# Causal pooling of three channel groups by transposes and doubled sums on VectorE in place of band products on TensorE, and a 0/1 product moved behind the inverses

## The chip, the cores and the metric

The kernel runs on one core of a Trainium2 chip. The metric is the device time of one execution in microseconds. Several executions are timed and their median is given; one more execution is taken by the hardware profiler, and all views of the profile and of its trace come from that one. Engines are named as in the profile: PE is TensorE (PEld its weight load), DVE is VectorE, ACT is ScalarE, POOL is GpSimd, SP is SyncE, which here issues most DMAs.

## What is computed

One layer of a decoder on 256 tokens of 2048 channels, float32 in and out. The part around the change is the token mixer: a normalised x is projected by `w_in` into q, k, v, z, two gates and a pooling input `p_in`. q, k and v go through a convolution over time and into a gated delta rule of 16 heads, whose output is `y_a`. The pooling input is cut into four groups of 512 channels with windows of 2, 4, 8 and 16 tokens:

```
def causal_multiscale_pool(u):          # u: (B, S, G, Cg)
    for gi, win in enumerate((2, 4, 8, 16)):
        hi = cs[:, 1:, gi]              # running sum up to t
        lo = cs[:, max(t + 1 - win, 0), gi]
        cnt = min(t + 1, win)
        outs.append((hi - lo) / cnt)
    return pooled - u                   # trailing mean minus the token itself

y_b   = einsum('bsgc,gcd->bsgd', pooled, pool_w) * pool_scale
mixed = sigmoid(g_a) * y_a + sigmoid(g_b) * y_b
x     = x + mixed @ w_out
```

After it come a second norm, a gated MLP with 5632 hidden channels and a last norm. They are not touched.

## The kernel before, in words

Large products. Every float32 weight is split into a high and a low part, so that three products of fp32r operands stand for one product in fp32. `weights()` gives out weight tiles of 256 x 512 (128 partitions x 1024) in one fixed order: the SP queue loads `raw` (L124, four buffers), ScalarE casts it to `whi` (L143, three buffers) and VectorE subtracts to get `wlo` (L151, three buffers), two tiles ahead of their use. `gemm_a` (L170) takes one tile per step and issues twelve products for it (L181 to L183), into `psm`, a PSUM tile with two buffers. Each step is two half-steps, and after each half-step it calls `side()`, which advances a generator of side work by one `yield`. The list `later` holds closures that `gemm_a` runs at its second step (c == 1): work on the result of the product before.

Order of a group. A loop over four groups g (L864), each with four heads and 512 pooling channels, runs these large products one after another: K, Q, V, P (the pooling input), GB (gate of the pooling branch), the pool product with `pool_w` (L916, two weight tiles), Z and GA. The result of P is evicted by ScalarE with the row scale into `e` (tag `ev`, one buffer, tokens on partitions), and `pooled` (L894) is put on `later`, so that it is traced at the second step of GB. The pool product needs its results `phi` and `plo` (high and low part, channels on partitions) as the stationary operand.

Pooling before. `pooled` multiplies `e` by a band matrix: `bands[:, g]` holds 1/win (1/count at the start, from `icnt`) on a band and subtracts the identity, all halved. For each pair of 128-channel blocks TensorE makes two fp32 products per block (L899 of 128 columns and L901 of 144), into a `psg` tile; ScalarE casts it to `phi` (L904) and VectorE subtracts to get `plo` (L905). `psg` is a PSUM tag with four buffers of one bank each, shared by all small products. `fixed_parts` (L534) builds the bands of all groups once, on GpSimd and VectorE, during group 0.

Side work. The generator `gdn` (L634) does the delta rule of a group: decay matrices, Gram products of k and q (L673, L675; two `psg` tiles per head, read by VectorE at L678 and L692 to L697), a way through DRAM for the 32 x 32 diagonal blocks (`cdd`, `lb`, L710 to L714), squares of q (L718), their block transpose and sum on VectorE (L722, L725), a product with a 0/1 matrix `sel` that sums them over partitions (L729) and four short VectorE operations that make `ro` of it (L733). After a fixed count of yields (`WAIT`, `LATE`) the inverses of the diagonal blocks follow on VectorE, a chain of 62 short operations (L744, L746) that reads `lb`, then a second way through DRAM (L751, L754), and then the products that merge the blocks and make the output (L788 to L847). `ro` is used near the end (L857). In group 3 the generator waits in a loop of yields (L769) until the last large product nears its end.

What sets the order. The kernel is traced under a tile framework (`TileContext(nc, schedule_with_timeline_sim=True)`), which tracks the dependences of tiles, hands out buffers and orders the instructions of each engine before the run by a simulated timeline; what is traced earlier goes first among what is ready. Within an engine the order is then fixed. Two stretches have an order on TensorE that is written out by hand: the start and the end of the mixer (L318, L926).

## Time and profile before

| what | value |
|---|---|
| median of 3 executions | 1565.36 us (1564.85 to 1565.47) |
| the profiled execution | 1565.06 us |
| its span in the trace | 1563.3 us |
| granted TensorE clock, mean | 0.998 |
| VectorE in the stretch 300.2 to 314.5 us | 10.51 us busy of 14.3 |
| VectorE in the stretch 476.5 to 493.5 us | 13.27 us busy of 17.0 |

The span is what the trace shows from the first to the last instruction; the profiled execution's own time is 1.8 us longer. A row of a timeline gives the start, the time from the first start to the last end, the engine, the line, the operation, output and inputs, the tile's shape and how often it follows itself. Successive matmuls overlap in the trace, so what one costs TensorE is read from the distance of starts. In the groups' rows stand the total busy time and the mean in ns of one, then the engine's idle time just before them with what ended it. Group 0 of the loop above lies between about 33 and 184 us, and the groups follow each other at about 179 us.

### The profile page before, as it was taken

Reading aid. Unit: us, or ns where it says so; the run is one execution under the profiler, and the core shown is the slowest. Engines: PE = TensorE matmul, PEld = TensorE weight load, DVE = VectorE, ACT = ScalarE, POOL = GpSimd, SP = SyncE. Lnnn points to the kernel's source line nnn. Section 1 sums busy time; section 2 is a strip of 40 time slices with the busy share of each in tenths; the row PEclk is TensorE's granted clock in tenths of the full one; section 3 lists DMA queues with packets and bytes.
Section 4 is the critical chain, followed back from the end, with each engine's and each line's share of the span. In section 5 each row is a group of like instructions: output and inputs, shape, how many; then the busy total and the mean of one; then the engine's idle time right before and its main releaser. Section 6 shows DMA issues by size and latency. Waiting matters only on the chain.

```text
span 1563.3 us, 21270 instructions
## 1 busy us (share of the span) xinstructions
PE 1554.1 (99%) x8008; PEld 1306.1 (84%) x8008; DVE 1085.6 (69%) x1702; ACT 745.7 (48%) x958; POOL 41.3 (3%) x69
## 2 busy tenths in 40 slices
PE   9999999999999999999999999999999999999997
PEld 8878888888888888888888888888888888888886
DVE  6898758896698848886656666776666667444444
ACT  6545445454554445354544544444444444333443
POOL 2110000000000001000000000000000000000000
PEclk9999999999999999999999999999999999999999
DMA  8676657676676656676656666666666666666662
GB/s 273 200 222 207 194 162 212 201 208 178 182 221 198 194 152 201 210 209 184 212 180 177 196 187 188 188 190 188 187 184 195 188 188 214 197 191 210 200 223 91
DMA packets 168229, 304.23 MB, mean 195 GB/s; under 512 B 19234, under 2 KB 22834, under 8 KB 167998
## 3 DMA queue, kind: packets, MB, share of 16 engines
q1 hardware_dynamic: 165104, 297.84, 64.0%
q10 hardware_dynamic: 3022, 5.03, 0.9%
q8 instruction: 63, 1.03, 0.3%
q14 instruction: 40, 0.33, 0.1%
HBM read 297.56 MB, written 5.27 MB: 194 GB/s over the span
## 4 chain that ended last, share of the span: by engine, by line
PE 99%; issue 1%; ACT 0%; DVE 0%; POOL 0%; POOLq 0%
PE psm L183 15%; PE psm L181 15%; PE psm L182 15%; PE psm L205 10%; PE psg L205 10%; PE psg L206 5%; PE psm L206 5%; PE psg L1058 3%; PE psg L1060 2%; PE psg L1059 2%; PE psm L1059 2%; PE psm L1060 2%; PE psm L1058 2%; PE psm L312 1%; PE psg L673 1%; PE psg L226 1%
## 5 line engine op out<-in xcount | busy, mean ns | idle before, releaser
L151 DVE TENSOR_TENSOR wlo<-raw,whi 128x1024 fp32r<-128x1024 f32 x522 | 636.7, 1223 | 374.1 <-ACT whi L143 371.2
L143 ACT CAST whi<-raw 128x1024 fp32r<-128x1024 f32 x524 | 551.1, 1053 | 715.7 <-PE psm L182 314.9
L183 PE MATMUL psm<-wlo,xhl 128*128 128x512 f32 x864 | 339.8, 393 | 0.0
L182 PE MATMUL psm<-whi,xhl 128*128 128x512 f32 x864 | 338.9, 392 | 0.0
L181 PE MATMUL psm<-whi,xhl 128*128 128x512 f32 x864 | 338.0, 391 | 0.0
L205 PE MATMUL psm<-fhl,whi 128*128 128x512 f32 x704 | 246.2, 396 | 0.0
L205 PE MATMUL psg<-fhl,whi 128*128 128x512 f32 x704 | 238.0, 394 | 0.0
L206 PE MATMUL psm<-fhl,wlo 128*128 128x256 f32 x704 | 194.4, 279 | 0.0
L183 PEld LDWEIGHTS psm<-wlo,xhl 128*128 128x128 f32 x864 | 162.3, 188 | 33.1
L182 PEld LDWEIGHTS psm<-whi,xhl 128*128 128x128 f32 x864 | 162.2, 188 | 33.1
L181 PEld LDWEIGHTS psm<-whi,xhl 128*128 128x128 f32 x864 | 162.2, 188 | 32.7
L206 PE MATMUL psg<-fhl,wlo 128*128 128x256 f32 x704 | 178.7, 279 | 0.0
L205 PEld LDWEIGHTS psm<-fhl,whi 128*128 128x128 f32 x704 | 131.4, 188 | 30.5
L205 PEld LDWEIGHTS psg<-fhl,whi 128*128 128x128 f32 x704 | 129.2, 188 | 24.2
L206 PEld LDWEIGHTS psg<-fhl,wlo 128*128 128x128 f32 x704 | 132.5, 188 | 6.9
L206 PEld LDWEIGHTS psm<-fhl,wlo 128*128 128x128 f32 x704 | 132.5, 188 | 1.1
L1058 PE MATMUL psg<-whi,hhi 128*128 128x512 f32 x168 | 65.5, 390 | 0.0
L1059 PE MATMUL psg<-whi,hlo 128*128 128x512 f32 x168 | 65.4, 389 | 0.0
L1058 PE MATMUL psm<-whi,hhi 128*128 128x512 f32 x168 | 65.4, 389 | 0.0
L1059 PE MATMUL psm<-whi,hlo 128*128 128x512 f32 x168 | 65.4, 389 | 0.0
L1060 PE MATMUL psm<-wlo,hhi 128*128 128x512 f32 x168 | 65.4, 389 | 0.0
L1060 PE MATMUL psg<-wlo,hhi 128*128 128x512 f32 x168 | 59.0, 389 | 0.0
(267 smaller groups left out, 1519.0 us busy)
## 6 DMA issues: line engine op xcount, KB each, us to landing
raw<-in_w_in_dram SPq DMA_DIRECT2D x224, 512.0 KB, 4.3
raw<-in_w_up_dram SPq DMA_DIRECT2D x176, 512.0 KB, 4.5
raw<-in_w_down_dram SPq DMA_DIRECT2D x88, 512.0 KB, 4.4
raw<-in_w_out_dram SPq DMA_DIRECT2D x32, 512.0 KB, 4.7
mv<-vrow SPq DMA_DIRECT2D x12, 512.0 KB, 5.6
taps<-in_conv_qkv_w_dram SPq DMA_DIRECT2D x16, 256.0 KB, 5.1
raw<-in_pool_w_dram SPq DMA_DIRECT2D x8, 512.0 KB, 4.5
vrow<-ev SPq DMA_DIRECT2D x4, 512.0 KB, 3.0
```

The costliest lines, as they stand in the source:

```text
L143: nc.scalar.copy(hi, raw)
L151: last_split[0] = nc.vector.tensor_tensor(lo, raw, hi.bitcast(F32), op=ALU.subtract).ins
L181: mm(ps[:, t, :], lh(k, t), hi[:, kk, :], start=(k == 0), stop=False)
L182: mm(ps[:, t, :], ll(k, t), hi[:, kk, :], start=False, stop=False)
L183: mm(ps[:, t, :], lh(k, t), lo[:, kk, :], start=False, stop=(k == nk - 1))
L205: mm(ps[f], hi[:, kk, fs], rhl(k), start=(k == 0), stop=False, skip_group_check=True)
L206: mm(ps[f][:, 1, :], lo[:, kk, fs], rhl(k)[:, 0, :], start=False, stop=(k == nk - 1), skip_group_check=True)
L226: nc.tensor.transpose(pt[:, ff, t * P : (t + 1) * P], src[:, t, f * P : (f + 1) * P], ident)
L312: mm(ps_k0[:, t, :], part(k, t), w[:, kk, :], start=(k == 0 and w is hi and part is xh), stop=(k == KD - 1 and w is lo))
L1058: mm(acc[c][t], lh(k, t), hi[:, kk, :], start=(k == 0), stop=False)
L1059: mm(acc[c][t], ll(k, t), hi[:, kk, :], start=False, stop=False)
L1060: mm(acc[c][t], lh(k, t), lo[:, kk, :], start=False, stop=(k == KF - 1))
```

## The change

For groups 0 to 2, `pooled` no longer multiplies by bands. It turns `e` by eight TensorE transposes into two `psg` tiles (`turned`, L218, the helper that the convolution uses too), ScalarE copies them to `u` (tag `pu`), and VectorE makes the window's sum by doubling: each step adds the running sum to itself shifted by n tokens, n = 1, 2, 4, while ScalarE copies the first n columns. One addition for a window of 2, two for 4, three for 8. Then VectorE multiplies the first `win` columns by 1/count, subtracts u there, and does the rest in one operation (sum/win - u); ScalarE casts the whole to `phi`, VectorE subtracts to get `plo`. Sums alternate between a new tag `pa` and the buffer that `plo` gets afterwards. Since the bands' factor of a half is gone, `e` is evicted with the halved row scale in these groups. Group 3 (window 16) keeps the band products, as `banded`, and `bands` holds its matrix alone. `plo` is allocated when the closure runs, and handed on in a list.

In `gdn`, the product with `sel` and the four operations of `ro` move from ahead of the wait for the inverses to behind the second way through DRAM, with one `yield` more after them. The tile `bat` at the start takes another tag.

```diff
--- before.py
+++ after.py
@@ -443,7 +443,6 @@
     for g, w in enumerate(WINDOWS):
         nc.vector.tensor_scalar(icnt[:, g, :], tio, float(w), None, op0=ALU.min)
     nc.vector.reciprocal(icnt, icnt)
-    nc.vector.tensor_scalar(icnt, icnt, 0.5, None, op0=ALU.mult)
     idh = mp.tile([P, P], F32, name="idh")
     nc.vector.tensor_scalar(idh, ident, 0.5, None, op0=ALU.mult)
 
@@ -464,7 +463,7 @@
         for kk in range(8):
             k = 8 * c + kk
             mm(pba, hi[:, kk, :], xhl[:, k], start=(k == 0), stop=(k == KD - 1))
-    bat = mp.tile([64, 2, S], F32, tag="u", name="bat")
+    bat = mp.tile([64, 2, S], F32, tag="w2", name="bat")
     nc.vector.tensor_copy(bat, pba[:64])
     pbt = pg([P, 2, 32])
     for t in range(2):
@@ -526,24 +525,23 @@
 
 
 
-    bands = mp.tile([P, 4, NB], F32, name="bands")
+    bands = mp.tile([P, NB], F32, name="bands")
 
     Ta = mp.tile([P, 8, P], F32, name="T")
     TTa = mp.tile([P, 8, P], F32, name="TT")
 
     def fixed_parts():
-        for g, win in enumerate(WINDOWS):
-            bd = bands[:, g, :]
-            nc.gpsimd.memset(bd, 0.5 / win)
-            nc.vector.tensor_copy(bd[:, 0:PAD], icnt[:, g, :])
-            for cs in (slice(0, P + PAD), slice(P + PAD, NB)):
-                b = bd[:, cs]
-                n = cs.stop - cs.start
-                nc.gpsimd.affine_select(b, b, pattern=[[1, n]], compare_op=ALU.is_ge, fill=0.0, base=0,
-                                        channel_multiplier=-1)
-                nc.gpsimd.affine_select(b, b, pattern=[[-1, n]], compare_op=ALU.is_ge, fill=0.0, base=win - 1,
-                                        channel_multiplier=1)
-                nc.vector.tensor_tensor(b[:, 0:P], b[:, 0:P], idh, op=ALU.subtract)
+        win = WINDOWS[3]
+        nc.gpsimd.memset(bands, 0.5 / win)
+        nc.vector.tensor_scalar(bands[:, 0:PAD], icnt[:, 3, :], 0.5, None, op0=ALU.mult)
+        for cs in (slice(0, P + PAD), slice(P + PAD, NB)):
+            b = bands[:, cs]
+            n = cs.stop - cs.start
+            nc.gpsimd.affine_select(b, b, pattern=[[1, n]], compare_op=ALU.is_ge, fill=0.0, base=0,
+                                    channel_multiplier=-1)
+            nc.gpsimd.affine_select(b, b, pattern=[[-1, n]], compare_op=ALU.is_ge, fill=0.0, base=win - 1,
+                                    channel_multiplier=1)
+            nc.vector.tensor_tensor(b[:, 0:P], b[:, 0:P], idh, op=ALU.subtract)
         nc.gpsimd.memset(Ta, 0.0)
         nc.gpsimd.memset(TTa, 0.0)
 
@@ -725,13 +723,6 @@
         nc.vector.tensor_reduce(qp.rearrange("p (h c) -> p h c", h=4), qx.rearrange("p h (c j) -> p h c j", j=32), axis=mybir.AxisListType.X,
                                 op=ALU.add)
         yield
-        pn = pg([P, 4, 2, 4])
-        mm(pn.rearrange("p h t c -> p (h t c)"), sel.rearrange("p b i -> p (b i)"), qp, start=True, stop=True)
-        ro = mp.tile([P, 2, 4], F32, tag="ro", name=nm("ro"))
-        for c in range(4):
-            pr = slice(32 * c, 32 * c + 32)
-            nc.vector.tensor_scalar(ro[pr], pn[pr, :, :, c].rearrange("p h t -> p t h"), EPS * P, EPS * EPS * P,
-                                    op0=ALU.mult, op1=ALU.add)
         for _ in range(WAIT - 3 + LATE[g]):
             yield
         tb = mp.tile([P, 8, B0], F32, tag="tb", name=nm("tb"))
@@ -752,6 +743,14 @@
         for r in range(NR):
             rs = slice(B0 * r, B0 * (r + 1))
             nc.sync.dma_start(TTa[rs, :, rs], tbd.rearrange("(q r) a (c i) -> r (a c) q i", q=8, i=B0)[r])
+        pn = pg([P, 4, 2, 4])
+        mm(pn.rearrange("p h t c -> p (h t c)"), sel.rearrange("p b i -> p (b i)"), qp, start=True, stop=True)
+        ro = mp.tile([P, 2, 4], F32, tag="ro", name=nm("ro"))
+        for c in range(4):
+            pr = slice(32 * c, 32 * c + 32)
+            nc.vector.tensor_scalar(ro[pr], pn[pr, :, :, c].rearrange("p h t -> p t h"), EPS * P, EPS * EPS * P,
+                                    op0=ALU.mult, op1=ALU.add)
+        yield
 
         for _ in conv:
             yield
@@ -887,24 +886,50 @@
         win = WINDOWS[g]
         psb = scales(g)
         ps = gemm_a(xh, xl, KD)
-        e = evict(ps)
+        e = evict(ps) if g == 3 else evict(ps, rsh)
         phi = mtile(g, [P, 4, S], F32R, nm("phi"))
-        plo = mtile(4 + g, [P, 4, S], F32R, nm("plo"))
-
-        def pooled(e=e, g=g, phi=phi, plo=plo):
+        plo = []
+
+        def banded(e=e, g=g, phi=phi, plo=plo):
+            plo.append(mtile(4 + g, [P, 4, S], F32R, nm("plo")))
             for f2 in range(2):
                 pt = pg([P, 2, S])
                 for ff in range(2):
                     fs = slice((2 * f2 + ff) * P, (2 * f2 + ff + 1) * P)
-                    mm(pt[:, ff, P:S], e[:, 1, fs], bands[:, g, P + PAD : NB], start=True, stop=False,
+                    mm(pt[:, ff, P:S], e[:, 1, fs], bands[:, P + PAD : NB], start=True, stop=False,
                        skip_group_check=True)
-                    mm(pt[:, ff, 0 : P + PAD], e[:, 0, fs], bands[:, g, 0 : P + PAD], start=False, stop=True,
+                    mm(pt[:, ff, 0 : P + PAD], e[:, 0, fs], bands[:, 0 : P + PAD], start=False, stop=True,
                        skip_group_check=True)
                 fs = slice(2 * f2, 2 * f2 + 2)
                 nc.scalar.copy(phi[:, fs, :], pt)
-                nc.vector.tensor_tensor(plo[:, fs, :], pt, phi[:, fs, :].bitcast(F32), op=ALU.subtract)
-
-        later.append(pooled)
+                nc.vector.tensor_tensor(plo[0][:, fs, :], pt, phi[:, fs, :].bitcast(F32), op=ALU.subtract)
+
+        def pooled(e=e, g=g, win=win, phi=phi, plo=plo):
+
+
+            u = mp.tile([P, 4, S], F32, tag="pu", name=nm("pu"))
+            for f2, pt in enumerate(turned(e)):
+                nc.scalar.copy(u[:, 2 * f2 : 2 * f2 + 2, :], pt)
+            src, n = u, 1
+            while n < win:
+                if n * 4 == win:
+                    dst = mp.tile([P, 4, S], F32, tag="pa", name=nm("pa"))
+                else:
+                    dst = mtile(4 + g, [P, 4, S], F32, nm("pb"))
+                nc.scalar.copy(dst[:, :, 0:n], src[:, :, 0:n])
+                nc.vector.tensor_tensor(dst[:, :, n:], src[:, :, n:], src[:, :, : S - n], op=ALU.add)
+                src, n = dst, 2 * n
+            pool = mp.tile([P, 4, S], F32, tag="pa", name=nm("pool"))
+            nc.vector.tensor_tensor(pool[:, :, 0:win], src[:, :, 0:win],
+                                    icnt[:, g, 0:win].unsqueeze(1).to_broadcast([P, 4, win]), op=ALU.mult)
+            nc.vector.tensor_tensor(pool[:, :, 0:win], pool[:, :, 0:win], u[:, :, 0:win], op=ALU.subtract)
+            nc.vector.scalar_tensor_tensor(pool[:, :, win:], src[:, :, win:], 1.0 / win, u[:, :, win:],
+                                           op0=ALU.mult, op1=ALU.subtract)
+            nc.scalar.copy(phi, pool)
+            plo.append(mtile(4 + g, [P, 4, S], F32R, nm("plo")))
+            nc.vector.tensor_tensor(plo[0], pool, phi.bitcast(F32), op=ALU.subtract)
+
+        later.append(banded if g == 3 else pooled)
 
         def gate(ps, tag):
             th = mp.tile([P, 2, 512], F32, tag=tag, name=nm("gate"))
@@ -913,7 +938,7 @@
             return th
 
         tb = gate(gemm_a(xh, xl, KD), "th")
-        ps = gemm_a(lambda k, t: phi[:, k, t * P : (t + 1) * P], lambda k, t: plo[:, k, t * P : (t + 1) * P], 4)
+        ps = gemm_a(lambda k, t: phi[:, k, t * P : (t + 1) * P], lambda k, t: plo[0][:, k, t * P : (t + 1) * P], 4)
         yb = mp.tile([P, 2, 512], F32, tag="yb", name=nm("yb"))
         nc.vector.tensor_tensor(yb, ps, psb.unsqueeze(1).to_broadcast([P, 2, 512]), op=ALU.mult)
         nc.vector.scalar_tensor_tensor(yb, tb, 1.0, yb, op0=ALU.add, op1=ALU.mult)
```

## Prediction

> **What bounds the kernel now.** I read the page from the top first: busy shares, the chain that ended last, and then the waits of TensorE alone.
>
> ```profile
> span 1563.3 us, 21270 instructions
> PE 1554.1 (99%) x8008; PEld 1306.1 (84%) x8008; DVE 1085.6 (69%) x1702; ACT 745.7 (48%) x958; POOL 41.3 (3%) x69
> ...
> PE 99%; issue 1%; ACT 0%; DVE 0%; POOL 0%; POOLq 0%
> ```
>
> ```profile
> PE psm L242 <- POOL ones L232: 1.1, 1, 1.1
> ```
>
> TensorE is busy 99% of the span, the chain that ended last lies on it for 99%, and the only wait of TensorE in the whole list of waits is 1.1 us at the very start. So the time is the sum of what TensorE is given, at the pace at which it takes instructions: a product less is time less, as long as no operand comes late. That pace is read from starts, since the durations of matmuls overlap. I therefore read two places of TensorE's timeline: eight transposes of an `ev` tile between large products, and the banded products of group 2.
>
> ```profile
> 250.53 0.39 PE L183 MATMUL psm<-wlo,xhl 128*128 128x512 f32 x1
> 250.76 1.03 PE L226 MATMUL psg<-ident,ev 128*128 128x128 f32 x8
> 251.55 0.48 PE L181 MATMUL psm<-whi,xhl 128*128 128x512 f32 x1
> 251.86 0.40 PE L182 MATMUL psm<-whi,xhl 128*128 128x512 f32 x1
> ```
>
> ```profile
> 480.71 0.39 PE L182 MATMUL psm<-whi,xhl 128*128 128x512 f32 x1
> 480.94 0.30 PE L729 MATMUL psg<-qp,sel 128*128 128x32 f32 x2
> 481.08 0.47 PE L899 MATMUL psg<-bands,ev 128*128 128x128 f32 x2
> ...
> 481.63 0.38 PE L899 MATMUL psg<-bands,ev 128*128 128x128 f32 x2
> ...
> 482.79 0.41 PE L901 MATMUL psg<-bands,ev 128*128 128x144 f32 x2
> 482.94 0.49 PE L183 MATMUL psm<-wlo,xhl 128*128 128x512 f32 x1
> 483.26 0.39 PE L181 MATMUL psm<-whi,xhl 128*128 128x512 f32 x1
> ```
>
> A large product starts 0.23 us after the one before it (480.71 to 480.94). From the large product ahead of a block to the second one behind it there are two such steps, and the rest is the block's price. Eight transposes: 251.86 - 250.53 = 1.33, less 0.45, is **0.88 us**. The product of q's squares with the banded products: 483.26 - 480.71 = 2.55, less 0.45, is **2.10 us**. Each fp32 product is two instructions here and a transpose is one: 16 against 8.
>
> **The change part by part.**
>
> *Products out, transposes in.* Of the 2.10 us, the product of q's squares (L729) takes 0.14 (480.94 to 481.08) and 0.08 more in the product behind it (0.47 against 0.38): 0.22, which leaves 1.88 for the banded ones. In groups 0 to 2 they go and eight transposes come: 1.88 - 0.88 = 1.00 us each, **3.0 us** in all. Group 3 keeps its bands.
>
> *L729 behind the inverses.* The same two instructions, now alone between large products. The trace has it only ahead of the bands. Bounds: 0.14 us as here, 0.88 us (the eight transposes) as the most. I take 0.22, nearest to its own row, so nothing per group; over four groups the bounds are -0.3 and +2.6. Its four short VectorE operations (ro) move along into the inverse stretch, where they add nothing new; ro is wanted only at the end of the recurrence. The added yield puts the later side work half a weight tile on, and group 3's loop that yields until the tail begins takes it up. No DMA changes its place in the SP queue, except that the value rows' work behind the inverse's transfers is issued one such step later.
>
> *VectorE, ScalarE, GpSimd.* Prices by these rows:
>
> ```profile
> L151 DVE TENSOR_TENSOR wlo<-raw,whi 128x1024 fp32r<-128x1024 f32 x522 | 636.7, 1223 | 374.1 <-ACT whi L143 371.2
> L143 ACT CAST whi<-raw 128x1024 fp32r<-128x1024 f32 x524 | 551.1, 1053 | 715.7 <-PE psm L182 314.9
> ```
>
> ```profile
> L628 DVE SCALAR_TENSOR_TENSOR kq<-th,cy 128x1024 f32<-128x1024 f32 x8 | 9.9, 1240 | 0.3 <-ACT th L627 0.3
> L905 DVE TENSOR_TENSOR plo<-psg,phi 128x512 fp32r<-128x512 f32 x8 | 5.2, 686 | 0.1
> L904 ACT CAST phi<-psg 128x512 fp32r<-128x512 f32 x8 | 4.7, 586 | 4.6 <-PE psg L901 4.6
> L733 DVE TENSOR_SCALAR ro<-psg 32x8 f32<-32x8 f32 x16 | 2.6, 162 | 0.5
> ```
>
> One doubling is 1.22 us (L151's size). The mean is two short operations of some 0.16 (L733) and one of 1.24 (L628), the low part 1.22 in place of two of 0.69. So VectorE gets 1.22n + 0.32 + 1.24 + 1.22 - 1.37 = 1.22n + 1.4 us more, n = 1, 2, 3: 2.6, 3.9 and 5.1. ScalarE copies u in two pieces (0.59 each, as phi before), makes short copies beside the additions (bounded by nothing and 0.59 each) and a phi of 1.05. Both have room over the span (69% and 48%), so none of this is on TensorE's path unless phi or plo is late for the pool product, or the new work holds up the weights queued behind it. Behind u's copies on ScalarE stand weight casts (715.7 us idle before them, mostly for TensorE to hand back a buffer), behind the doublings on VectorE the splits (374.1 us idle, for the casts): that idle time is the cover, and without it each microsecond of chain would be one of TensorE's. The band work that goes at the start was off the path too, by the one wait of 1.1 us.
>
> *Is phi late?* The pool products of groups 0, 1 and 2 begin here, the second with the start of its group's bands:
>
> ```profile
> 135.43 0.39 PE L181 MATMUL psm<-whi,phi 128*128 128x512 f32 x1
> ```
>
> ```profile
> 304.76 0.47 PE L899 MATMUL psg<-bands,ev 128*128 128x128 f32 x2
> ...
> 314.46 0.39 PE L181 MATMUL psm<-whi,phi 128*128 128x512 f32 x1
> ```
>
> ```profile
> 493.50 0.39 PE L181 MATMUL psm<-whi,phi 128*128 128x512 f32 x1
> ```
>
> And this is VectorE ahead of them, in the same order:
>
> ```profile
> 122.72 1.20 DVE L725 TENSOR_REDUCE qp<-kq 128x32 f32<-128x1024 f32 x1
> ```
>
> ```profile
> 299.71 0.48 DVE L697 SCALAR_TENSOR_TENSOR ga<-psg,sj,dec 128x256 f32<-128x256 f32 x1
> ...
> 301.33 1.21 DVE L725 TENSOR_REDUCE qp<-kq 128x32 f32<-128x1024 f32 x1
> 302.46 2.35 DVE L151 TENSOR_TENSOR wlo<-raw,whi 128x1024 fp32r<-128x1024 f32 x2
> ...
> 311.22 0.28 DVE L741 COPY tb<-idb 128x256 f32<-128x256 f32 x1
> 313.12 0.42 DVE L744 TENSOR_TENSOR tmp<-lb,tb 128x248 f32<-128x248 f32 x1 [1.62 <-DMA lb<-cdd]
> ```
>
> ```profile
> 476.03 0.48 DVE L697 SCALAR_TENSOR_TENSOR ga<-psg,sj,dec 128x256 f32<-128x256 f32 x1
> ...
> 477.65 1.21 DVE L725 TENSOR_REDUCE qp<-kq 128x32 f32<-128x1024 f32 x1
> 478.78 2.35 DVE L151 TENSOR_TENSOR wlo<-raw,whi 128x1024 fp32r<-128x1024 f32 x2
> 481.28 0.69 DVE L733 TENSOR_SCALAR ro<-psg 32x8 f32<-32x8 f32 x4
> 482.00 1.23 DVE L151 TENSOR_TENSOR wlo<-raw,whi 128x1024 fp32r<-128x1024 f32 x1
> ...
> 486.40 1.23 DVE L151 TENSOR_TENSOR wlo<-raw,whi 128x1024 fp32r<-128x1024 f32 x1 [1.85 <-ACT whi L143]
> 487.54 0.28 DVE L741 COPY tb<-idb 128x256 f32<-128x256 f32 x1
> ```
>
> The four psg banks are held by the Gram products until L697 reads them. Two are free at 476.5, yet the bands start at 481.08, right behind L729, which needs L725's sums. I read this as L729 holding its turn for a bank ahead of them; with L729 gone, the transposes can go at 476.6. Group 2 then: transposes to 477.4, copies of u to 478.1, VectorE free of L725 at 478.8, three additions, two short operations and the mean in 5.2 us, and up to three weight splits among them, 3.6 us: 487.6. phi on ScalarE to 488.9, plo to 490.1. The pool product starts 1.2 us earlier than before (2.10 - 0.88), at 492.3: **2.2 us to spare**. Group 1 alike from 302.5: 4.0 + 3.6 gives 310.1, phi 311.4, plo 312.6, against 313.3: **0.7 us to spare**. Group 0 has one addition less: from 123.9 its 2.8 + 3.6 give 130.3, plo 132.8, against 134.2. So I forecast no new wait.
>
> **Sum.** The profiled execution took 1565.06 us (span 1563.3 and 1.8 around it), 0.3 under the median of 1565.36. Less 3.0 that is 1562.1, or 1562.4 by the median; I say 1562.2.
>
> **The rivals.**
>
> *The pooled operand is a little late.* If the transposes stay where the bands were (the reading of the banks is wrong, or the order planned for TensorE keeps them there), the chain starts 4 us later: in group 1, from L729's turn at 304.6, u is there at 306.2, four us of chain and two splits end at 312.6, plo at 315.1 against 313.5: 1.6 us late. By the same working groups 0 and 2 lose 0.5 and nothing. Net -3.0 + 2.1: **1564.2**. For it: the row at 313.12, where VectorE stands 1.62 us for the transfer of lb; whatever is queued behind waits too, plo among it. Against it: the banks are free early.
>
> *VectorE's order starves the chain: slower.* VectorE works in order, and inverse, splits and doublings now meet in one stretch. If two other operations come between every two of the chain, it runs at a third of its pace: group 2's 5.2 us become 15.6, phi's low part is there at 496.9 against 492.5; group 1's 12.0 from 302.5 give 317.0 against 313.5; group 0 loses 0.4. TensorE stands 8.3 us: net +5.3, **1570.6**. It decides from 3.0 us of standing, a chain at some 2.2 times its length. For it: the inverse's operations (L741 at 487.54) start inside the stretch already. Against it: at 486.40 VectorE stood 1.85 us for want of a cast, so it was ahead of its work.
>
> *Transposes are no cheaper.*
>
> ```profile
> L226 PE MATMUL psg<-ident,ev x64: 270/272/307, 62.6 to 605.2; 128*128 128x128 f32 x64
> ```
>
> If TensorE paid a transpose's full 0.27 us, eight would take 2.2 us against 1.88, and the time would be 1565.06 + 3 x 0.3 = **1566.0**. The row at 250.76 speaks against it: the next large product starts 0.79 us later. The Trainium skill (TensorE: Matmul & The Clock Gate, Part 4: PE-mode transpose) gives about 275 ns for one in a kernel and says that the clock gate does not count transposes as work. By that figure the change would lose 0.9 us; the trace agrees with it as a duration (272 ns), not as a pace (eight in 1.03 us).
>
> **How the numbers follow.** Forecast: 0.60, 1561.6 to 1562.9 (the bound of -0.3, the median's 0.3, and how side products happen to group). Late operand: 0.17. Starved chain: 0.18. Dear transposes: 0.02. A gain above 3.5 us: 0.03. The range runs from 1561.4 to 1566.0; it leaves out most of the starved chain and a little below. About what a measurement of this kernel can tell from no change is 0.2%, 3.1 us, and 1565.36 - 3.1 = 1562.2 cuts the forecast's own case in two. Faster by more: 0.33 + 0.03 = 0.36. Within: 0.27 + 0.17 + 0.02 and 0.02 of the starved chain, 0.48. Slower by more: 0.16.
>
> **What would show it.** Right: blocks of eight L226 on `ev` in the gate product of groups 0 to 2, at 0.88 us each and some 4 us earlier than the bands; L729 alone, behind the inverses, at 0.2; TensorE's list of waits as short as now; phi done over 1 us before the pool product. Wrong: TensorE waiting at the product that reads phi or plo, or at L183 for a wlo; L744's wait for lb ahead of plo; transposes still at the bands' place.

## The result, and the profile after

The changed kernel takes **1576.86 us** (median of 4 runs, 1575.42 to 1580.69) against 1565.41 us before (1564.85 to 1565.71): 11.45 us more, a ratio of 1.0075 with a 95% interval of 1.0063 to 1.0087. The forecast was 1562.2 us, with a range up to 1566.0. The profiled execution took 1580.69 us. Its page begins:

```profile
span 1579.0 us, 21230 instructions
...
PE 1560.6 (99%) x7984; PEld 1309.0 (83%) x7984; DVE 1092.6 (69%) x1704; ACT 749.0 (47%) x967; POOL 47.3 (3%) x54
...
PE 96%; DMA 2%; DVE 1%; issue 1%; SPq 1%; ACT 0%; POOLq 0%; POOL 0%; DVEq 0%
```

The busy shares are as before. What differs is the chain that ended last: 3% more of it has left TensorE, for a DMA above all. TensorE's list of waits, one row long before, says where:

```profile
PE psm L181 <- ACT phi L928: 3.6, 2, 2.0
PE psg L787 <- DVE T L764: 3.2, 2, 2.5
PE psm L182 <- DVE plo L930: 2.0, 2, 1.0
```

That is 8.8 us of waiting, in three places: ahead of the pool products of groups 1 and 2 (phi, then plo), and ahead of group 3's U product (the first product that reads T, the transposed inverses). Group 1's place in TensorE's timeline (start, duration, line):

```profile
312.35 0.39 PE L183 MATMUL psm<-wlo,xhl 128*128 128x512 f32 x1
314.35 0.50 PE L181 MATMUL psm<-whi,phi 128*128 128x512 f32 x1 [1.62 <-ACT phi L928]
315.87 0.79 PE L182 MATMUL psm<-whi,plo 128*128 128x512 f32 x1 [1.02 <-DVE plo L930]
316.46 0.63 PE L183 MATMUL psm<-wlo,phi 128*128 128x512 f32 x1
316.89 0.63 PE L181 MATMUL psm<-whi,phi 128*128 128x512 f32 x1
```

From start to start there are 2.00 and 1.52 us where 0.23 is the pace: 3.1 us of standing (time in which TensorE has nothing that it could start). Behind it the products do not return to their pace but follow each other at 0.43 us. The stretches of the same time show why (columns: busy time with instructions, granted clock, DMA share, GB/s); first after, then before:

```profile
312.00:316.00 4.00, 1.36 (x6) 0.89 0.67 214
316.00:322.00 6.00, 6.00 (x15) 0.50 0.50 166
322.00:328.00 6.00, 6.00 (x28) 1.00 0.41 126
```

```profile
316.00:322.00 6.00, 6.00 (x28) 1.00 0.66 182
```

15 products in place of 28 in six busy microseconds: the granted clock is at 0.50. In fine stretches it is so from 315.1 to 322.0, from 499.5 to 506.3 and from 731.6 to 738.4: each time 6.8 us. It begins while TensorE still stands (at 315.1, where plo's product starts at 315.87), so a part of it costs nothing. "PE 99%" doesn't show it, for a slow product counts as busy.

Set against before by the starts of the large products, the profiled run's 15.6 us are: group 0, gate product to pool product, -0.95; group 1, gate product to Z, +5.1; group 2 the same, +5.2; group 3, last gate product to output product, +6.3. Adding back the gain of 0.95 in groups 1 and 2 and taking off the standing (3.1, 3.4 and 3.3 us by starts) leaves 3.0, 2.7 and 3.0 us for the half clock. The other runs took 1575.4 to 1577.3, at a mean clock of 0.994 and 0.995 in place of 0.992: an estimated 6 to 9 us less at half clock (0.002 to 0.003 of 1579 us, doubled).

This is VectorE ahead of group 1's pool product, and then SyncE's queue in the same time:

```profile
306.16 1.22 DVE L920 TENSOR_TENSOR pa<-pu 128x1020 f32<-128x1020 f32 x1
307.49 1.22 DVE L920 TENSOR_TENSOR pb<-pa 128x1016 f32<-128x1016 f32 x1
308.62 1.22 DVE L151 TENSOR_TENSOR wlo<-raw,whi 128x1024 fp32r<-128x1024 f32 x1
...
310.04 1.20 DVE L926 SCALAR_TENSOR_TENSOR pool<-pb,pu 128x1008 f32<-128x1008 f32 x1
312.72 0.42 DVE L735 TENSOR_TENSOR tmp<-lb,tb 128x248 f32<-128x248 f32 x1 [1.47 <-DMA lb<-cdd]
313.05 0.17 DVE L925 TENSOR_TENSOR pool<-pool,pu 128x16 f32<-128x16 f32 x1
313.14 1.22 DVE L151 TENSOR_TENSOR wlo<-raw,whi 128x1024 fp32r<-128x1024 f32 x1
314.27 0.41 DVE L737 TENSOR_TENSOR tb<-tb,tmp 128x248 f32<-128x248 f32 x1
314.60 1.22 DVE L930 TENSOR_TENSOR plo<-pool,phi 128x1024 fp32r<-128x1024 f32 x1
```

```profile
304.41 0.39 SPq L124 DMA_DIRECT2D raw<-in_pool_w_dram  x1
304.89 0.41 SPq L124 DMA_DIRECT2D raw<-in_w_in_dram  x1
305.54 1.73 SPq L712 DMA_DIRECT2D lb<-cdd  x4
```

The chain is nearly done at 311.2. But its last piece, the short subtraction of 0.17 us (L925), is queued behind the first operation of the inverse (L735), which stands 1.47 us for lb; then come a split and L737, and only then plo. In group 2 it is the same: L735 stands 1.83 us, with four operations of the pooling behind it. Before the change that wait was there too (1.62 us), with nothing behind it that TensorE was near to needing. And lb, itself four transfers of 128 KB, was fetched behind two weight tiles of 512 KB; it landed 5.6 us after its issue.

The theory to test: lb's wait on VectorE makes phi and plo late; the standing halves the clock; and group 2's longer stretch pushes group 3's T past a place written by hand. Rivals: the moved 0/1 product is to blame; the chain is too long whoever waits in it; the standing of all groups adds up in group 3.

### The profile page after: what moved, and what is told of

It reads as the page before. It is cut to its first block, busy times and chain, and to the rows that moved or that the text cites. A ratio compares the mean times of both kernels' runs of the same rounds, so it can differ in the third digit from the quotient of the medians.

```text
span 1579.0 us, 21230 instructions
## 1 busy us (share of the span) xinstructions
PE 1560.6 (99%) x7984; PEld 1309.0 (83%) x7984; DVE 1092.6 (69%) x1704; ACT 749.0 (47%) x967; POOL 47.3 (3%) x54
## 4 chain that ended last, share of the span: by engine, by line
PE 96%; DMA 2%; DVE 1%; issue 1%; SPq 1%; ACT 0%; POOLq 0%; POOL 0%; DVEq 0%
PE psm L182 14%; PE psm L183 14%; PE psm L181 14%; PE psm L205 10%; PE psg L205 10%; PE psg L206 5%; PE psm L206 5%; PE psg L1083 2%; PE psg L1085 2%; PE psg L1084 2%; PE psm L1083 2%; PE psm L1085 2%; PE psm L1084 2%; PE psm L312 1%; PE psg L671 1%
## 5 line engine op out<-in xcount | busy, mean ns | idle before, releaser
L205 PEld LDWEIGHTS psg<-fhl,whi 128*128 128x128 f32 x704 | 129.2, 188 | 24.1
```

The lines of the kernel that those rows point to most:

```text
L205: mm(ps[f], hi[:, kk, fs], rhl(k), start=(k == 0), stop=False, skip_group_check=True)
```

## The experiments

Before, run beside them, took 1565.5 to 1565.9 us (medians).

**The moved product alone.** On before:

```diff
- pn = pg([P, 4, 2, 4]); mm(pn..., sel..., qp, ...); ro = ...
  for _ in range(WAIT - 3 + LATE[g]):
...
      nc.sync.dma_start(TTa[rs, :, rs], tbd...)
+ pn = pg([P, 4, 2, 4]); mm(pn..., sel..., qp, ...); ro = ...
+ yield
```

> The kernel before, with one part of the change: the product of q's squares and its four short operations (ro) stand behind the inverses; the pooling stays with the bands. Main theory (the VectorE stretch ahead of the pool product makes phi and plo late): this part is free, within 1 us of before, 1564.5 to 1566.5 us, no wait of TensorE for phi, plo or T and no stretch at a granted clock of 0.5. Rival (the move itself pushes the inverses or the recurrence back): some of the 11.5 us that the whole change lost appear here, 1568 us or more, with TensorE standing ahead of group 3's U product.

1565.72 us, ratio 0.9999 (0.999 to 1.0008), no new wait: by itself this part is free. It also tests a reading of the prediction, that L729 holds a PSUM bank ahead of the bands. Group 2's first band product in this run:

```profile
480.49 0.38 PE L900 MATMUL psg<-bands,ev 128*128 128x128 f32 x2
```

It was at 481.08: 0.6 us earlier, not 4.5. What does hold it there isn't shown; TensorE waits for nothing ahead of it, so it can only be the planned order.

**Groups apart.** The other groups' bands are kept; the second run has `(2,)` here, the third `(0,)`.

```diff
- later.append(banded if g == 3 else pooled)
+ later.append(pooled if g in (0, 1) else banded)
```

> The change with groups 2 and 3 kept on the bands, groups 0 and 1 pooled on VectorE. Main theory: group 0 gains 0.95 us, group 1 gains 0.95 us of products and loses about 3.5 us of standing for phi and plo and some 3.4 us at the half clock behind it; groups 2 and 3 as before, since the standstill ahead of group 3's U product comes from group 2. Sum +5: about 1570 us (1568 to 1572). Rival A (lateness of each pooled group carries on to group 3): its U product stands too, 1575 us. Rival B (the half clock has nothing to do with the standing): 1567 us, TensorE standing in group 1 with the clock at 1.0 behind it.

1569.33 us, ratio 1.0024 (1.0014 to 1.0034). Group 1 stands 2.26 and 1.52 us from start to start, with 6.8 us at half clock behind; groups 2 and 3 are as before.

> The change with groups 0, 1 and 3 on the bands, group 2 alone pooled on VectorE. Main theory: group 2 saves 0.95 us of products, loses about 3.9 us of standing for phi and plo and 3.4 us at the half clock; and its longer stretch on VectorE puts off group 3's second Gram products and inverse, so that group 3's U product stands some 3 us for T, with a half clock behind it again: together +9 to +12, 1574 to 1577 us. Rival (group 3's standing is the sum of what all three groups lost): group 3 stands by less than 1 us, 1571 us.

1572.57 us, ratio 1.0042 (1.0029 to 1.0056), a little under the forecast: group 2's half clock lasted 3.4 us, not 6.8. Group 3's stand needs group 2 alone:

```profile
PE psg L790 <- DVE T L767: 3.2, 2, 2.6
PE psm L181 <- ACT phi L931: 1.6, 1, 1.6
...
PE psm L182 <- DVE plo L933: 1.0, 1, 1.0
```

> Group 0 alone pooled on VectorE, groups 1 to 3 on the bands (whose building at the start is put on GpSimd). Main theory (group 0 has no inverse of an earlier group in its stretch and starts its transposes 19 products earlier, so nothing of it is late): -0.95 us, 1564.9 us (1564.5 to 1565.5), no stand for phi, plo or T. Rival (VectorE's extra 2.6 us anywhere ahead of the recurrence sets group 1 to 3 back): 1566.5 us or more.

1564.92 us, ratio 0.9999 (0.999 to 1.0008); in the profiled run the gain of 0.95 is there at group 0's pool product, and 0.9 of it is lost again from group 3's pool product on, in small waits for low parts.

**lb at once.**

```diff
- nc.sync.dma_start(cdd[...], gt[rs, :, rs])
...
- nc.sync.dma_start(lb[...], cdd...)
+ nc.gpsimd.memset(lb, 0.0)
```

> The changed kernel, with the way of the diagonal blocks through DRAM left out: lb is filled with zeros on GpSimd, so the inverses are those of identity blocks (that part of the computation is left out). The planned order of all engines stays that of the changed kernel. Main theory (VectorE stands in front of the first inverse operation for lb, 1.47 us in group 1 and 1.83 us in group 2, and the pooling's last operations are queued behind it): standing for phi falls from 2.0 to about 0.5 us in group 1 and from 2.35 to about 0.5 in group 2, plo's 1.5 us stays, group 3's T comes about 1.8 us sooner; 1566 to 1573 us. Rival (the chain itself is too long for its place, whoever waits in it): phi as late as in the changed kernel, 1575 us or more.

1565.23 us, ratio 0.9996 (0.9987 to 1.0004): better than forecast, 11.6 us less than the changed kernel and level with before. phi is on time in both groups, plo 1.3 us late, T on time, no half clock. But this version leaves the diagonal blocks out: the transfers are gone too, and the inverses begin sooner.

**What a stand costs.** On before, work added on VectorE at five weight tiles of the down projection.

```diff
  last_split[0] = nc.vector.tensor_tensor(lo, raw, hi.bitcast(F32), op=ALU.subtract).ins
+ for n in MORE.get(len(made), ()):
+     nc.vector.tensor_tensor(lo[:, 0:n], raw[:, 0:n], hi[:, 0:n].bitcast(F32), op=ALU.subtract)
```

> The kernel before with repeats of the low-part subtraction on VectorE at five weight tiles of the down projection, 2 to 3 us apart in size: by the slack of a tile (3.6 us) and 1.14 us a repeat, TensorE stands once each for about 0.95, 1.6, 2.1, 2.7 and 3.2 us, 10.5 us in all. The result is the same. It measures what a stand of TensorE costs behind itself. Main theory (a stand or two close stands of about 2 us and more are followed by a granted clock of 0.5, in stretches of 3.4 us, which cost 1.7 us each): stands of 0.95 and 1.6 are followed by nothing, 2.1 and more by 3.4 to 6.8 us at 0.5; time 1565.9 + 10.5 + 5 to 10, 1581 to 1587 us. Rival A (only a stand of 3 us and more halves the clock): 1578 to 1580 us. Rival B (the half clock needs the two stands with one product between): none of the five, 1576.4 us.

1568.14 us: a miss. The planned order laid the repeats into idle time; the longest step was 1.30 us, and nothing followed.

```diff
+ if m: nc.vector.tensor_reduce(jr, hi[:, 0, 0:32]...to_broadcast([P, 32, m]), ...)
  last_split[0] = nc.vector.tensor_tensor(lo, raw, hi.bitcast(F32), op=ALU.subtract).ins
```

> In place of the spread repeats, which the planned order laid into VectorE's idle time, one long sum of 4096, 4608, 5120, 5632 and 6144 elements a partition on VectorE ahead of the low-part subtraction of five weight tiles of the down projection (the result is the same). By 1.21 us for 1024 elements each takes 4.4 to 6.6 us, and by a slack of 3.6 us between the low part and its first product TensorE stands for about 0.8, 1.35, 1.9, 2.4 and 3.0 us, 9.5 us in all, each stand alone and ended by one product's operand. Main theory: the stands of 0.8 and 1.35 are followed by nothing, those of 1.9 and more by stretches at a granted clock of 0.5 of 3.4 us or twice that (1.7 or 3.4 us lost): 1565.6 + 9.5 + 5 to 10, 1580 to 1585 us. Rival A (only a stand of about 3 us halves the clock): 1577 to 1579 us. Rival B (no single stand does, it takes two with one product between): 1575 us.

1568.18 us: smaller than meant again. The longest stand came behind the sum of 6.55 us, 2.15 us from start to start. The clock stayed at 1.00:

```profile
1438.57 0.50 PE L1068 MATMUL psm<-wlo,hhi 128*128 128x512 f32 x1 [1.76 <-DVE wlo L159]
```

So this single stand of 1.9 us cost only itself; where the line is, the other runs tell (below).

**Z in between.**

```diff
- srcs += cols(pool_w[0, g], 0, 4)
+ srcs += cols(w_in[0], C_Z + 512 * g, KD) + cols(pool_w[0, g], 0, 4)
...
- nc.vector.tensor_tensor(dst[:, :, n:], src[:, :, n:], src[:, :, : S - n], op=ALU.add)
+ nc.gpsimd.tensor_tensor(dst[:, :, n:], src[:, :, n:], src[:, :, : S - n], op=ALU.add)
```

> The changed kernel with the Z gate's product ahead of the pool product in every group (its weight tiles are read in that order), which gives the pooled operand 22 us more, and the doubled sums and the last subtraction on GpSimd, the scaling by 1/win on ScalarE, so that VectorE gets little more than before. Main theory (the change lost time by an operand too late for its place, and by VectorE's extra work ahead of group 3's inverse, not by its products): no stand for phi, plo or T, the three gains of 0.95 us stay: 1565.9 - 2.9 = 1563.0 us (1562.3 to 1564). Rival (GpSimd's additions are so much slower than VectorE's, or slow VectorE, that phi is late again or the weights' splits are): 1566 us or more, TensorE standing for phi or for a low part.

1566.87 us, ratio 1.0009 (1.0 to 1.0018): phi and plo are no longer waited for, as both theories of lateness have it, but four low parts are, 2.0 us together. VectorE and GpSimd in group 1:

```profile
307.96 2.13 DVE L151 TENSOR_TENSOR wlo<-raw,whi 128x1024 fp32r<-128x1024 f32 x1 [2.06 <-ACT whi L143]
...
312.12 2.29 DVE L735 TENSOR_TENSOR tmp<-lb,tb 128x248 f32<-128x248 f32 x1 [1.81 <-DMA lb<-cdd]
```

```profile
307.12 1.88 POOL L920 TENSOR_TENSOR pb<-pa 128x1016 f32<-128x1016 f32 x1
...
311.73 2.40 POOL L926 TENSOR_TENSOR pool<-pool,pu 128x1024 f32<-128x1024 f32 x1 [1.57 <-ACT pool L925]
```

Operations of 1.22 and 0.42 us end at 310.09 and 314.41, 1.1 and 0.3 us after GpSimd's. The rival is right: what leaves VectorE comes back as blocking.

> Z ahead of the pool product in groups 1 and 2 alone, with their doubled sums on GpSimd; group 0 as in the changed kernel, group 3 as before. In the earlier run with Z in between, VectorE's operations beside a GpSimd addition took 2.13 us for 1.22 and 2.29 us for 0.42, and the low parts behind them came late (2.0 us of standing). Main theory (VectorE and GpSimd shut one another out, and the two groups that overlap an inverse pay for it): group 0 -0.95, groups 1 and 2 about +0.3 each against before: 1565 to 1566 us, no version that beats before by more than a microsecond. Rival (the loss lay in group 0 or in the order of group 3's tiles): 1563.5 us or less.

1566.80 us, ratio 1.0009 (1.0 to 1.0018), 0.8 us over the forecast; low parts are 2.4 us late in all, 1.9 of them in groups 1 and 2, so these two carry most of that loss.

**The order of waiting.**

```diff
- with tc.issue_after(last_split[0]):
+ with tc.issue_after(last_split[0]), tc.issue_after(pool_last[0]):
      nc.vector.tensor_copy(tb, idb)
```

> The changed kernel with the first work of the inverses on VectorE queued behind plo, so that the wait for lb cannot stand ahead of the pooling. In the planned order this moves group 2's recurrence back by some 15 large products, and with it group 2's transposes (from product 46 to 71 of the gate product). Main theory (the wait for lb is the price in group 1, a late start in group 2): in group 1 phi is on time and plo 1.3 us late, no half clock, 5 us less lost there than in the changed kernel; in group 2 the chain starts 5 us later and phi is 3 to 5 us late, with a half clock; group 3's T late by 3 us as before. 1573 to 1577 us. Rival (lb alone is at fault, in both groups): 1568 us or less.

1574.41 us, ratio 1.0057 (1.0045 to 1.007). Group 1 loses 0.7 us to plo and no clock; group 2's chain, planned later, makes phi 4.7 us late. The lateness has only moved.

**U later.**

```diff
- ps = gemm_a(xh, xl, KD, range(6))
+ ps = gemm_a(xh, xl, KD, range(7))
  ending.append(True)
```

> The changed kernel with group 3's U product 12 large products (some 2.7 us) later in its hand-written place in the last gate product. The stands of groups 1 and 2 stay. Main theory (T is 2.9 us late for that place, and that is all that group 3 loses): the stand of 2.65 + 0.65 us goes to under 1 us, and the half clock behind it with it: 5 to 6 us less than the changed kernel, about 1571 us (1570 to 1573). Rival (the recurrence behind T is itself the end: what TensorE doesn't stand ahead of U it stands at the close of the recurrence): 1575 us or more, TensorE standing for another operand ahead of the output product's close.

1571.91 us, ratio 1.0045 (1.0033 to 1.0058), 5.0 less than the changed kernel: from the last gate product to the first output product it takes 0.4 us more than before, not 6.3. Later in the output product, at 770 us, TensorE waits 1.1 us for the result of group 3 (`mhi`, `mlo`), as the rival had it in small. So T was late for its place, and what stands behind it was late by much less.

**lb sooner, the whole computation kept.** First on two queues:

```diff
- nc.sync.dma_start(cdd[...], gt[rs, :, rs])
+ (nc.sync if t == 0 else nc.gpsimd).dma_start(cdd[...], gt[rs, :, rs])
```

> The changed kernel complete, with one edit: of the eight transfers that take the diagonal blocks to DRAM (4.5 us of issuing on SyncE, one behind the other), four are issued on GpSimd's queue, so that lb can be fetched some 2 us sooner. TensorE's planned order stays that of the changed kernel. Main theory (lb's lateness on VectorE is the root in groups 1 and 2, and the half clock follows from the standing): lb is there 1.5 to 2.5 us sooner, phi is on time or under 0.5 us late, plo 1.3 us late, T under 1.5 us late, no half clock: 1565 to 1568 us. Rival (in the run with zeros for lb it was the missing transfers, or the inverse's earlier start, that healed it): phi is late by 1 us and more as in the changed kernel, 1574 us or more.

1580.48 us, ratio 1.0089 (1.0072 to 1.0105): a miss that says more than a hit. With four fewer issues ahead of them, three weight tiles went out ahead of lb, and lb came later, 7.4 us after its issue in place of 5.6:

```profile
310.94 0.17 DVE L925 TENSOR_TENSOR pool<-pool,pu 128x16 f32<-128x16 f32 x1
315.25 0.42 DVE L735 TENSOR_TENSOR tmp<-lb,tb 128x248 f32<-128x248 f32 x1 [4.15 <-DMA lb<-cdd]
```

L925 now stands ahead of L735, and phi is on time in group 1; plo stands behind it and comes 5.7 us late. What is queued behind L735 is late, what is ahead is not.

> Groups 0 and 1 pooled on VectorE, groups 2 and 3 on the bands, and the diagonal blocks' transfers on two queues as in the run beside it; in the planned order of group 1 the short subtraction now stands ahead of the first inverse operation. Main theory: group 0 -0.95; group 1 -0.95 and up to 1.3 us of standing for plo; nothing in groups 2 and 3: 1565.6 - 0.6 = 1565.0 us (1563.7 to 1566). Rival (group 1's chain is late also without the wait for lb): 1567 us or more, with TensorE standing for phi.

1571.82 us, ratio 1.0039 (1.0026 to 1.0051), a miss too, the same in small: L738 stands 2.23 us for lb, phi is on time and plo 3.8 us late.

Then the right lever, SyncE's order:

```diff
- last_load[0] = nc.sync.dma_start(raw[:, k], src[:, k]).ins
+ with tc.issue_after(last_lb[0]) if len(loads) in pool_tiles else ExitStack():
+     last_load[0] = nc.sync.dma_start(raw[:, k], src[:, k]).ins
```

> The changed kernel complete, with one edit in SyncE's queue: the second weight tile of each pool product is fetched behind lb instead of ahead of it (in the changed kernel one or two transfers of 512 KB were issued 1 us ahead of lb's and shared the DMA engines with it). The planned order of TensorE and VectorE stays that of the changed kernel. Main theory (lb's arrival is what holds the pooling's last operations, and the half clock follows from the standing): lb is there 1 to 3 us sooner; phi under 0.5 us late, plo 1.3 us late in groups 1 and 2, T on time or under 1 us late, no half clock: 1565 to 1567 us. Rival (what healed it with lb at once was the inverse's missing transfers, not the wait): 1573 us or more, phi late by over 1 us though lb came sooner. If lb doesn't come sooner, neither is told apart.

**1568.13 us**, ratio 1.002 (1.0011 to 1.003): 8.7 us less than the changed kernel, with every product, operation and transfer kept, though 1.1 us over the forecast. In group 1 the weight tile ahead of lb, and those behind it, are issued 3.7 us later. lb itself is issued 0.8 us later than in the changed kernel and is there sooner, 2.6 us after its issue in place of 5.6. SyncE's queue, VectorE, TensorE's waits and ScalarE:

```profile
306.34 1.71 SPq L715 DMA_DIRECT2D lb<-cdd  x4
308.09 0.42 SPq L127 DMA_DIRECT2D raw<-in_pool_w_dram  x1
```

```profile
311.47 0.41 DVE L738 TENSOR_TENSOR tmp<-lb,tb 128x248 f32<-128x248 f32 x1
311.80 0.17 DVE L928 TENSOR_TENSOR pool<-pool,pu 128x16 f32<-128x16 f32 x1
```

```profile
PE psm L185 <- DVE plo L933: 2.5, 2, 1.3
PE psm L184 <- ACT phi L931: 1.2, 2, 0.8
...
PE psg L790 <- DVE T L767: 0.4, 1, 0.4
```

```profile
311.83 1.05 ACT L146 CAST whi<-raw 128x1024 fp32r<-128x1024 f32 x1 [3.26 <-DMA raw<-in_pool_w_dram]
312.78 1.04 ACT L931 CAST phi<-pool 128x1024 fp32r<-128x1024 f32 x1
```

L738 doesn't wait, T is 0.4 us late, and in the profiled run, the only one with a trace, the clock is never halved (four others show a mean clock of 0.997 in place of 0.998). phi is still 1.0 and 0.5 us late, but not by the chain's length: the pooling is done at 311.97, and ScalarE stands 3.26 us for the weight tile that this edit put back, with phi's cast queued behind it (2.88 us in group 2). With lb at once, and no tile put back, phi was on time. The rival "chain too long" holds for plo alone, which takes VectorE 1.22 us behind phi and was 1.3 us late there. Some 2.5 and 2.1 us of standing are left here of 3.1 and 3.4: most of the gain is the half clock, which no longer comes, and T, which is nearly on time.

> Groups 0 and 1 pooled on VectorE, groups 2 and 3 on the bands, lb fetched ahead of the pool product's second weight tile. Main theory: group 0 -0.95; group 1 -0.95 and 1.3 us of standing for plo; nothing else: 1565.6 - 0.6 = 1565.0 us (1564 to 1566.5), against 1569.3 with the same groups and lb behind the weights. Rival: 1568 us or more.

1568.79 us, ratio 1.0018 (1.0009 to 1.0027), a miss in the rival's range, no half clock in the profiled run; phi 0.85 and plo 1.55 us late (forecast 1.3 in all), phi again behind a weight cast that stands 3.1 us for its tile, and 1.5 us more in small steps of group 3.

The third and fourth run have this besides, for `nk == 4`:

```diff
  mm(ps[:, t, :], lh(k, t), hi[:, kk, :], ...)
- mm(ps[:, t, :], ll(k, t), hi[:, kk, :], ...)
  mm(ps[:, t, :], lh(k, t), lo[:, kk, :], ...)
...
+ for kk in range(2):
+     for t in range(2):
+         mm(ps[:, t, :], ll(2 * c + kk, t), hi[:, kk, :], ...)
```

> As the run beside it (groups 0 and 1 pooled on VectorE, lb ahead of the weights), and in each weight tile of the pool products the eight products with phi stand ahead of the four with plo, so that plo is wanted 1.8 us after phi and not 0.23. Main theory (only plo's 1.3 us are left of the loss): no stand in group 1, both gains of 0.95 us stay: 1563.7 us (1563 to 1565). Rival (the planned order of the later groups moves with it and gives it back): 1566 us or more, with stands in group 2 or 3.

**1563.96 us**, ratio 0.999 (0.9981 to 0.9999): 1.6 us less than before and 12.9 less than the changed kernel, the only version here whose interval lies below 1, and by little. plo is wanted eight products after phi and has come by then:

```profile
PE psm L252 <- POOL ones L242: 1.1, 1, 1.1
PE psm L184 <- ACT phi L941: 0.8, 1, 0.8
```

> The whole change with lb ahead of the weights and the products with phi first in the pool products. Main theory: no stand for phi or plo over 0.3 us in any group, T at most 1 us late: 1565.6 - 2.9 + 0 to 1.5 = 1562.7 to 1564.5 us. Rival (in the planned order group 3's second Gram products still slip behind group 3's value product, and its U product stands 3 us for T, with the half clock behind it): 1567 to 1570 us.

1570.75 us, ratio 1.0034 (1.0021 to 1.0047), a miss, and neither theory: T is 0.4 us late, but in the planned order of this version group 2's transposes come 13 products later, and phi is 4.1 us late with 6.8 us of half clock.

## Why the prediction was wrong, point by point

- *What bounds the kernel.* Right, and no help: a total says nothing of a wait that isn't there yet.
- *Products out, transposes in, -1.00 us each.* Right. In group 0 TensorE's timeline shows it without disturbance:

```profile
121.15 0.39 PE L181 MATMUL psm<-whi,xhl 128*128 128x512 f32 x1
121.38 1.03 PE L226 MATMUL psg<-ident,ev 128*128 128x128 f32 x8
122.17 0.48 PE L182 MATMUL psm<-whi,xhl 128*128 128x512 f32 x1
122.49 0.39 PE L183 MATMUL psm<-wlo,xhl 128*128 128x512 f32 x1
```

  122.49 - 121.15 less two steps is 0.88, as priced, and the pool product comes 0.95 us sooner. *Transposes no cheaper* falls with it.
- *L729 costs nothing.* Right by itself: 1565.72 us. But in groups 1 and 2 of the changed kernel it does not stand behind the inverses: it starts at 304.59 and 486.31, and the four operations of `ro`, 0.68 us of VectorE at 305.45 and 487.25, stand directly ahead of the first addition. What they cost there wasn't tried alone.
- *Prices on VectorE.* Right: 1.22 us a doubling, 1.20 the mean, 1.22 the low part.
- *"Both have room over the span (69% and 48%)" and the 374.1 us of idle as cover.* Wrong. Cover has to lie in the stretch and in the order: in group 1 the only idle time between the mean and phi was one wait, and it lay inside the chain.
- *"I read this as L729 holding its turn for a bank ahead of them; with L729 gone, the transposes can go at 476.6."* **This step failed first.** L729 wasn't what held them (480.49 in the run above). In the changed kernel group 2's transposes start at 484.75, in a gate product that began 4.5 us later than before, so 3.7 us later than I put them. The margins of 2.2 and 0.7 us were gone with it: with lb at once and the transposes as late, plo was 1.3 us late in groups 1 and 2, which ate the forecast gain (1565.23). No run had the transposes sooner.
- *"So I forecast no new wait."* **The step that failed in size.** I had the row with lb's 1.62 us and named plo behind it, but priced it only as a rival, with the wait itself left out of the sum. It was 1.47 and 1.83 us, in front of phi as well, and it took the standing from 1.3 us a group to 3.1 and 3.4. The half clock that follows such a standing was no term of the sum at all. Together with group 3 that is the 11.6 us between lb at once and the changed kernel. The last part had "L744's wait for lb ahead of plo" among the signs of being wrong; it is the one that came.
- *The rivals.* "A little late" had the place right but stopped at 2.1 us of standing. "Starved chain" had the sign, at 1570.6, but its mechanism was other operations between those of the chain, where it was one wait for a transfer. That its 8.3 us of standing are near the 8.8 measured is luck: it put them all ahead of the pool products, where 5.6 were measured. What neither had: 8.7 us lost to the half clock in the profiled run, and group 3.
- *Group 3* was left out because it keeps its bands. Its U product has a place written by hand, with little room: before, T was made by 718.24 and wanted at 719.23.

```profile
716.40 1.84 DVE L765 STREAM_TRANSPOSE T<-TT 32x256 f32<-32x256 f32 x4 [3.14 <-DMA TT<-tbd]
...
719.23 0.69 PE L788 MATMUL psg<-T,ga 32*32 32x32 f32 x32
```

  Groups 0 and 1 pooled leave that alone, group 2 alone breaks it, lb ahead mends it. Through which operations group 2's extra work reached group 3's inverse wasn't tried one by one. The trace shows its second Gram products behind the start of the gate product instead of ahead of it; but so does the run with lb ahead, where T is only 0.4 us late. There the first operation that reads lb starts 21.6 us behind the start of the gate product, against 24.1 in the changed kernel and 18.3 before. So lb's way is a part of T's lateness too.

## What to carry to other kernels

An engine's idle share is not cover: list what stands in its queue between the inputs of your new chain and its end, with the wait of each, and count an existing harmless wait as part of the chain. An order or a place that was fitted to the old times (a hand-written slot, a queue of transfers) belongs in the sum even where the change doesn't touch it. And when an in-order engine stands for a transfer, look at which large ones were issued just ahead of it: that cost more here than all the products saved. Putting the large one back has a price of its own, on the engine that reads it: here ScalarE stood for it, with phi behind.

## What the runs showed of the hardware

The clock behind a stand. The standing is the sum, within a few microseconds, of what the steps have over the pace:

| standing, us | where | time at 0.5 |
|---|---|---|
| 1.3 | lb at once, groups 1 and 2 | none |
| 1.9 | five blocks | none |
| 2.5 | lb ahead, group 1; U later, group 2 | none |
| 3.0 | group 2 alone; U later, group 1 | 3.4 us |
| 3.1, 3.4 | changed kernel, groups 1 and 2 | 6.8 us |
| 3.4, 5.7 | two queues, groups 2 and 1 | 3.4 us, 6.8 us |
| 3.8 | two queues, groups 0 and 1 | 3.4 us |
| 4.2 | phi first, all groups, group 2 | 6.8 us |
| 4.9 | inverse behind, group 2 | 3.4 us |

In these traces a standing of up to 2.5 us cost itself. From 3.0 on there were one or two pieces of 3.4 us at half clock behind it, whose number doesn't follow the size; each costs at most 1.7 us, less where it begins within the standing. One standing of 3.3 us (inverse behind, group 3) had none. Pairs with a product between (3.0 to 3.4 us) had it, and so had single stands of 3.8 us and more; between 1.9 and 3.8 no single stand at large products alone was measured. The Trainium skill (TensorE: Matmul & The Clock Gate, Part 1, What's actually happening) says that activity is judged in free-running windows of 3413 ns; the pieces agree, and such windows would scatter as these do.

VectorE and GpSimd. Operations with two inputs took 2.13 for 1.22 us and 2.29 for 0.42 beside additions on GpSimd. The Trainium skill (SBUF — State Buffer, SBUF: two separate sides) has it that the two engines' shared ports are locked for a whole instruction by the one that starts first; the trace agrees: GpSimd's began first, and VectorE's ended 1.1 and 0.3 us after them.

Issuing and landing. In group 1 of the changed kernel the eight transfers of 16 KB to `cdd` took SyncE 4.54 us to issue, 0.33 to 0.43 us each and 1.31 the last, and lb's own four 1.73 us. lb landed 2.6 us after its issue with both weight tiles behind it, 5.6 us with two ahead of it and 7.4 us with three.
